# Gate and up products of all experts as float32 products in halves of TensorE's columns, weights unsplit, a ring of six slots

## The chip, the cores and the metric

The kernel runs on one core of a Trainium2 chip. A core has TensorE (PE; PEld is its loading of stationary tiles), VectorE (DVE), ScalarE (ACT), GpSimd (POOL) and a queue that issues loads (SP). The metric is the device time of one execution in microseconds (us); the median of the runs shown for the kernel before is 1627.42 us.

## What is computed

Two transformer blocks on 256 tokens of width 1024, all in float32. The first ends in a mixture of 32 experts (width 512, weights `w1`, `w3`, `w2`), the second block has two layers, each ending in a mixture of 16 experts (width 256). Each token goes to two experts. Cut to what matters here:

```python
# first block: 32 experts, D_FF_EXPERT = 512
return (jax.nn.silu(xb @ w1[e]) * (xb @ w3[e])) @ w2[e]
# second block, both layers: 16 experts, D_EXPERT = 256
a = jax.nn.silu(t @ w_gate[e]) * (t @ w_up[e])
out = out + combine[:, e:e + 1] * (a @ w_down[e])
```

In front of each mixture stand a norm, the routing and the mixer of the layer; between the first mixture and the last stand a latent attention and a long convolution, whose filters (the functions with `filter` in their names) are computed early, while the first mixture runs.

## The kernel before

Each expert has room for 64 tokens (`CAP`); what does not fit goes through a loop at the end (`overflow`), taken only where an expert has more. I call the stage of the 32 experts the wide stage and the other two the narrow stages.

**Streaming.** The weights come through a ring of slots, each 2 MB (128 partitions x 4096 float32). In the wide stage an expert takes three: gate, up, and half of the down weights of an earlier pair of experts. A narrow expert's gate and up share one slot, and a pair's down weights take one. `Stream.get` hands out a slot and issues the loads that are due, on SP's queue. The ring has four slots (the wide one uses one more place once, at the start).

**Gather.** For four experts at a time (`GE`) a product with a one-hot matrix picks their tokens, in 8 pieces of the contraction (`gather`, L254). The tokens are kept as a high and a low part, side by side: 64 columns of high and 64 of low make the 128 columns of a stationary tile.

**Gate and up.** A unit is two pieces of the contraction of one weight matrix, 512 columns each. `split` makes the high part of the weights on ScalarE (L272) and the low part on VectorE (L274); `mm` then runs four float32r products for a unit (L280). The result has the high tokens' and the low tokens' share in separate rows; `turn` (L307) adds them and transposes, in four float32 products with a 128x64 matrix `S`. Then come `silu` (L315) and the product with the up half, `act` (L322).

**Down and out.** The down product (L357) runs two experts at once: each has 64 tokens, and one expert's go to the lower, the other's to the upper half of the array's columns, as float32 products straight from the ring. `out_hi` (L364) and `out_lo` (L371) weight and split the result, `scatter` (L379) adds it to the tokens with a float32r product. `slots` (L334) makes the matrix for that.

**Order.** In `run` the order of all this is written by hand: `seq` lists the units, and a table (`LATE`, `OUT`, `OUTL`, `END`) says after how many further units each follow-up stands. The products' split runs `LA` = 2 units ahead. All other work, the filter rounds of the long convolution among it (L1630, L1649, L1657 on TensorE, sixteen rounds), is put between by a scheduler. Products of the mixture share three PSUM banks (`bank`), the filter rounds have one (`fill`).

Of the kernel before, what the change touches and what calls it, by code (L numbers as in the profile page):

```python
# [31 lines left out]
XG = 10  # L32
PRW, PRN = 2, 2
LA = 2
# [53 lines left out]
def make_consts(k):  # L88
# [15 lines left out]

    k.S = k.t(c, [P, CAP], F32, "S")
    nc.vector.tensor_tensor(k.S, k.ident[:, :CAP], k.ident[:, CAP:], op=ALU.add)
# [121 lines left out]
class Moe:  # L228


    def __init__(self, k, es, name, r, h2h, h2l, load, NE, FF):
        self.k, self.nc, self.r = k, k.nc, r
        self.h2h, self.h2l = h2h, h2l
        self.load = load
        self.NE, self.FF, self.name = NE, FF, name
        self.sb = es.enter_context(k.pool(name + "sb", 2))
        self.acc = [[k.acc() for h in range(2)] for t in range(2)]
        self.first = True
        self.xg, self.oh, self.st = {}, {}, {}
        self.prime = PRW if FF == 512 else PRN  # L240
# [5 lines left out]
    def gather(self, g, c, oh=None, n=None):  # L246
# [3 lines left out]
        pm = k.bank()  # L250
# [5 lines left out]
        self.gp = pm  # L256
        return i

    def gathered(self, g, c, n=None):
        k, nc, pm = self.k, self.nc, self.gp  # L260
        n = n or GE
        N = n * CAP
        xg = k.t(self.sb, [P, n, 2, CAP], F32R, "xg", bufs=XG)
        self.gathers = nc.scalar.activation(xg.rearrange("p e a s -> p a e s"),  # L264
                             pm[:, :2 * N].rearrange("p (a e s) -> p a e s", a=2, e=n), AF.Copy)
        self.xg[g][c] = xg
# [10 lines left out]
    def mm(self, out, lhs, parts, start, stop):  # L277
        for j in range(2):
            for a, w in enumerate(parts):
                self.nc.tensor.matmul(out, lhs[j].bitcast(w.dtype), w[:, j, :], start=(start and j == 0 and a == 0),  # L280
                                      stop=(stop and j == 1 and w is parts[-1]))
# [4 lines left out]
    def x_of(self, e, c):  # L286
        g, i = divmod(e, GE)
        return self.xg[g][c][:, i].rearrange("p a s -> p (a s)")

    def up_unit(self, e, kind, u, parts):  # L290
# [6 lines left out]
    def evac(self, e, kind):  # L297
        s = self.state(e)
        s["s" + kind] = self.k.t(self.sb, [P, 512], F32, "s" + kind)
        self.nc.scalar.activation(s["s" + kind], s["p" + kind], AF.Copy)  # L300

    def turn(self, e, kind, c0, n):
# [6 lines left out]
        s["t" + kind] = pm  # L309

    def silu(self, e):
        s = self.state(e)
        n = self.FF // P
        s["sg"] = self.k.t(self.sb, [P, n * CAP], F32, "sg")
        self.nc.scalar.activation(s["sg"], s["tg"][:, :n * CAP], AF.Silu)  # L315

    def act(self, e):
        s, k, nc = self.state(e), self.k, self.nc
        n = self.FF // P
        pu = s["tu"][:, :256] if self.FF == 512 else s["tg"][:, n * CAP:2 * n * CAP]  # L320
        s["av"] = k.t(self.sb, [P, n, CAP], F32, "a", bufs=3)
        nc.vector.tensor_tensor(s["av"].rearrange("p c s -> p (c s)"), pu, s["sg"], op=ALU.mult)  # L322
# [62 lines left out]
    def overflow(self, add):  # L385
# [4 lines left out]
        with k.tc.If(r.nblk > 0):  # L390
            with k.tc.For_i(0, r.nblk, 1):
# [34 lines left out]
                x_of = lambda c: self.xg[g][c][:, 0].rearrange("p a s -> p (a s)")  # L426

                def units(kind, u):
                    w = k.t(self.sb, [P, 2, 512], F32, "wh", bufs=LA + 2)
# [3 lines left out]
                for kind in ("g", "u") if wide else ("g",):  # L433
                    s["p" + kind] = k.bank()
                    for u in range(4):
                        self.mm(s["p" + kind], [x_of(2 * u), x_of(2 * u + 1)], self.split(units(kind, u)), u == 0, u == 3)
                    self.evac(e, kind)
                    self.turn(e, kind, 0, 4)
                    if kind == "g":
                        self.silu(e)  # L440
# [29 lines left out]
    def start(self, oh):  # L470

        self.onehot(0, oh)
        with self.k.tc.issue_after(self.low.ins):
            self.parts = {("g", 0, u): self.split(self.load("g", 0, u)) for u in range(self.prime)}
        with self.k.tc.issue_after(self.high.ins):
            for c in range(8):
                self.ready = self.gather(0, c)
                self.gathered(0, c)

    def run(self):  # L480
# [4 lines left out]
        LATE = (1, 2, 3, 3) if wide else (2, 2, 3, 4)  # L485
        OUTL = (1, 2, 4) if wide else (1, 1, 4)
        END, OUT = (0, 0, 0, 0), (1, 2, 4) if wide else (1, 1, 4)
        seq = []
        for i in range(NE + 2):
            if i < NE:  # L490
                for kind in ("g", "u") if wide else ("g",):
                    seq += [(kind, i, u) for u in range(4)]
# [9 lines left out]
        for e in range(NE):  # L502

            late = END if e == NE - 1 else LATE
            for kind in ("g", "u") if wide else ("g",):
                n = where[kind, e, 3]
                lt = LATE if kind == "g" and wide else late
                add(n + lt[0], self.evac, e, kind)
                add(n + lt[1], self.turn, e, kind, 0, 4)
                if kind == "g":  # L510
                    add(n + lt[2], self.silu, e)
                if kind == "u" or not wide:
                    add(n + lt[3], self.act, e)
            ge = where["g", e, 3]
            if e % 2 == 0:
                n = ge if wide else ge - 1
                add(n, self.slots, e // 2)
                add(n + 1, self.slots_out, e // 2)
                for h in range(2):
                    d = where["d", e // 2, h * nck + nck - 1]  # L520
                    o = OUTL if e == NE - 2 else OUT
                    add(d + o[0], self.out_hi, e // 2, h)
                    add(d + o[1], self.out_lo, e // 2, h)
                    add(d + o[2], self.scatter, e // 2, h)
        for g in range(1, NE // GE):
            el = g * GE - 1
            last = "u" if wide else "g"
            early = XG - 8
            add(where[last, el - 1, 0], self.onehot, g)
            ns = [where[last, el - 1, 1 + c] for c in range(early)]  # L530
# [1830 lines left out]
```

## Time and profile before

| | us |
|---|---|
| median of 3 runs (lowest to highest) | 1627.42 (1626.41 to 1630.23) |
| the profiled execution, its own time | 1621.13 |
| its span, first to last instruction | 1619.4 |
| wide stage, first gate product to the last pair's down product | 336.27 to 925.12 |
| first narrow stage | 1114 to 1251 |
| second narrow stage | 1469 to 1608 |

The page gives busy time by engine, what ended an engine's idle time, and the queues. A record of TensorE is one pass as the profiler wrote it: a float32r product is one record, a float32 product is two. A record's duration includes the time that its result takes to come through, so records overlap; the price of one is read from the distance of starts. Times of a group are the union of its records. In a window's row the engines stand as PE, PEld, DVE, ACT, POOL, then the granted clock of TensorE; in a group's row the idle time behind the second bar is that of the engine just before the group's instructions, with what ended it.

### The profile page before, as it was taken

To read this page: it belongs to the slowest core of one execution; us is meant where nothing else is said; L and a number is where in the kernel's file an instruction comes from. 1 tells how busy PE (TensorE), PEld (TensorE's weight loads), DVE (VectorE), ACT (ScalarE), POOL (GpSimd) and SP (SyncE) were. 2 spreads that over 40 slices of the span, in tenths; PEclk is the share of its full clock that TensorE was granted. 3 is DMA by queue.
4 is the path that set the end of the run, shared out by engine and by line. 5 is a ranking of instruction groups with operands and counts; after the bars stand their busy time and mean duration, and the time that the engine had idled before them with its cause. 6 is when DMAs were issued, how large, how long until landed. Compare 5 with 4: busy or idle time off the path is not lost. (4 is left out here: it accounts for less than half of the span.)

```text
span 1619.4 us, 20894 instructions
## 1 busy us (share of the span) xinstructions
PE 1477.1 (91%) x7754; PEld 1014.0 (63%) x7754; DVE 1004.8 (62%) x1935; ACT 889.6 (55%) x1413; POOL 70.5 (4%) x98
## 2 busy tenths in 40 slices
PE   5898999889999999999999969997999799878997
PEld 2675586666665666666666544656676678556764
DVE  3553564687657565656565567447775768567665
ACT  2462343476666666666656444436775534337774
POOL 0000000110000000000000000001000000010000
PEclk8899999989999999999999989997999899978999
DMA  8557714658988889888889667665997674475994
GB/s 326 177 169 239 258 44 143 273 223 321 370 342 327 349 316 358 319 347 329 333 340 384 278 257 282 211 245 226 355 366 298 244 268 154 131 299 196 365 362 155
DMA packets 67789, 444.48 MB, mean 274 GB/s; under 512 B 7813, under 2 KB 8165, under 8 KB 43744
## 3 DMA queue, kind: packets, MB, share of 16 engines
q1 hardware_dynamic: 61712, 424.97, 69.4%
q0 software_dynamic: 5536, 17.37, 3.0%
q8 instruction: 63, 1.03, 0.3%
q10 hardware_dynamic: 432, 0.72, 0.1%
q14 instruction: 46, 0.38, 0.1%
HBM read 437.75 MB, written 5.29 MB: 274 GB/s over the span
## 5 line engine op out<-in xcount | busy, mean ns | idle before, releaser
L274 DVE TENSOR_TENSOR wl<-ring,wh 128x1024 fp32r<-128x1024 f32 x384 | 454.4, 1220 | 130.8 <-ACT wh L272 129.2
L272 ACT ACTIVATE wh<-ring 128x1024 fp32r<-128x1024 f32 x384 | 386.1, 1053 | 14.3 <-DVE h2l L1926 13.3
L280 PE MATMUL bank<-wl,xg 128*128 128x512 f32 x768 | 315.6, 411 | 16.2 <-DVE wl L274 16.1
L280 PE MATMUL bank<-wh,xg 128*128 128x512 f32 x768 | 311.2, 405 | 3.0 <-ACT wh L272 3.0
L280 PEld LDWEIGHTS bank<-wl,xg 128*128 128x128 f32 x768 | 145.4, 189 | 72.0 <-DVE wl L274 42.5
L357 PE MATMUL bank<-ring,a 128*64 128x512 f32 x768 | 188.6, 605 | 0.0
L280 PEld LDWEIGHTS bank<-wh,xg 128*128 128x128 f32 x768 | 145.8, 190 | 42.6 <-issue 14.6
L812 DVE TENSOR_TENSOR wl<-ra,wh 128x1024 fp32r<-128x1024 f32 (+1 forms) x77 | 93.5, 1216 | 81.3 <-ACT wh L810 69.2
L810 ACT ACTIVATE wh<-ra 128x1024 fp32r<-128x1024 f32 (+1 forms) x77 | 80.7, 1054 | 111.1 <-PE acc L825 38.1
L264 ACT ACTIVATE xg<-bank 128x512 fp32r<-128x512 f32 x128 | 75.5, 597 | 58.2 <-PE bank L254 56.1
L357 PEld LDWEIGHTS bank<-ring,a 128*64 128x64 f32 x768 | 47.6, 136 | 74.4 <-issue 61.6
L893 PE MATMUL fill<-rb,cpad 128*32 128x512 f32 x384 | 84.5, 620 | 8.1 <-DMA rb<-in_w_mod_dram 4.5
L307 PEld LDWEIGHTS bank<-S,sg 128*128 128x128 f32 x512 | 65.1, 191 | 18.1 <-ACT wh L272 11.4
L307 PE MATMUL bank<-S,sg 128*128 128x64 f32 x512 | 66.2, 272 | 0.4 <-ACT sg L300 0.2
L364 ACT ACTIVATE o_h<-bank,gt 128x512 fp32r<-128x512 f32 x64 | 43.7, 683 | 36.1 <-PE bank L357 36.1
L254 PE MATMUL bank<-oh,h2h 128*128 128x256 f32 x256 | 60.6, 322 | 3.1 <-DVE oh L222 2.5
L315 ACT ACTIVATE sg<-bank 128x256 f32<-128x256 f32 (+1 forms) x64 | 21.2, 332 | 71.1 <-PE bank L307 68.6
L1632 DVE TENSOR_TENSOR hd<-fill,dec 128x512 f32<-128x512 f32 x16 | 11.0, 690 | 79.2 <-PE fill L1630 79.2
L254 PEld LDWEIGHTS bank<-oh,h2h 128*128 128x128 f32 x256 | 46.6, 210 | 17.3 <-ACT xg L264 6.9
L1683 PE MATMUL acc<-hTh,wh 128*128 128x256 f32 x192 | 56.0, 293 | 0.0
L1683 PE MATMUL acc<-hTl,wh 128*128 128x256 f32 x192 | 55.9, 293 | 0.0
L254 PE MATMUL bank<-oh,h2l 128*128 128x256 f32 x256 | 54.8, 300 | 0.6 <-DVE h2l L1926 0.6
(666 smaller groups left out, 2526.0 us busy)
## 6 DMA issues: line engine op xcount, KB each, us to landing
ring<-in_w_dram SPq DMA_DIRECT2D x64, 2048.0 KB, 9.0
ring<-in_moe_w_in_dram SPq DMA_DIRECT2D x32, 2048.0 KB, 9.6
ring<-in_w_dram SPq DMA_DIRECT2D x62, 1024.0 KB, 8.2
rb<-in_ada_w_dram SPq DMA_DIRECT2D x96, 512.0 KB, 4.6
ring<-in_moe_w_down_dram SPq DMA_DIRECT2D x32, 1024.0 KB, 9.0
rb<-in_w_mod_dram SPq DMA_DIRECT2D x32, 512.0 KB, 4.5
ra<-in_hy_w_in_dram SPq DMA_DIRECT2D x12, 1024.0 KB, 6.9
ra<-in_w_in_dram SPq DMA_DIRECT2D x20, 512.0 KB, 3.7
```

The costliest lines, as they stand in the source:

```text
L254: i = nc.tensor.matmul(pm[:, a * N:(a + 1) * N], h[:, t, c * P:(c + 1) * P], oh[:, t], start=(t == 0), stop=(t == 1))
L264: self.gathers = nc.scalar.activation(xg.rearrange("p e a s -> p a e s"), pm[:, :2 * N].rearrange("p (a e s) -> p a e s", a=2, e=n), AF.Copy)
L272: self.high = nc.scalar.activation(wh, w, AF.Copy)
L274: nc.vector.tensor_tensor(wl, w, wh.bitcast(F32), op=ALU.subtract)
L280: self.nc.tensor.matmul(out, lhs[j].bitcast(w.dtype), w[:, j, :], start=(start and j == 0 and a == 0), stop=(stop and j == 1 and w is part ...
L307: self.nc.tensor.matmul(pm[:, c * CAP:(c + 1) * CAP], s["s" + kind][:, c0 + c * P:c0 + (c + 1) * P], k.S, start=True, stop=True)
L357: self.nc.tensor.matmul(q["d", h][i * CAP:(i + 1) * CAP], self.state(2 * p + i)["av"][:, c], w[:, i], start=(c == 0), stop=(c == nk - 1))
L364: nc.scalar.activation(oh[r], s["d", h][r], AF.Copy, scale=s["gt"][r])
L810: k.last[0] = k.nc.scalar.activation(wh[:, :, :n], w, AF.Copy)
L812: k.last[1] = k.nc.vector.tensor_tensor(wl[:, :, :n], w, wh[:, :, :n].bitcast(F32), op=ALU.subtract)
L893: nc.tensor.matmul(pr[32 * g:32 * g + 32], k.cpad[:, l, 2 * q + i], wq[:, i], start=(r == 0), stop=(r == 1))
L1683: nc.tensor.matmul(acc[i][:, :T], y[:, jj, i * P:(i + 1) * P], self.hT[x][:, kt], start=(kt == 0 and a == 0), stop=(kt == 7 and a == 2))
```

## The change

Gate and up become float32 products. For each piece of the contraction the same stationary tile, 64 columns of unsplit tokens, is used twice: for the gate weights into rows 0 to 63 of a PSUM bank, that is into the lower half of the array's columns, and for the up weights into rows 64 to 127, the upper half. The weights are read from the ring as they are; `split` and `mm` are gone, and with them `LA`, the primed units at the start, and the `wh` and `wl` buffers. The host lays `w1` and `w3` out together as `w13`, so that a slot of the wide ring holds gate and up of half an expert's contraction.

The gather adds high and low in PSUM (four products into the same columns), and evicts two pieces at a time. One `evac` and one `turn` serve gate and up: four 128x128 transposes in the wide stage, two in the narrow ones. The order table is replaced: eviction right after an expert's last unit, turn, silu and act two units later, gather pieces one per unit in the last two experts of a group. The rings have six slots in all three stages. Padding and sides of some buffers change.

```diff
     def gather(self, g, c, oh=None, n=None):
...
+        o = c % 2 * 256
+        if o == 0:
+            self.gp = k.bank()
         for a, h in enumerate((self.h2h, self.h2l)):
             for t in range(2):
-                i = nc.tensor.matmul(pm[:, a * N:(a + 1) * N], h[:, t, c * P:(c + 1) * P],
-                                     oh[:, t], start=(t == 0), stop=(t == 1))
+                i = nc.tensor.matmul(self.gp[:, o:o + N], h[:, t, c * P:(c + 1) * P],
+                                     oh[:, t], start=(a == t == 0), stop=(a == t == 1))
...
-    def split(self, w):
-        k, nc = self.k, self.nc
-        wh = k.t(self.sb, [P, 2, 512], F32R, "wh", bufs=LA + 2)
-        self.high = nc.scalar.activation(wh, w, AF.Copy)
-        wl = k.t(self.sb, [P, 2, 512], F32R, "wl", bufs=LA + 2)
-        nc.vector.tensor_tensor(wl, w, wh.bitcast(F32), op=ALU.subtract)
-        return wh, wl
...
+    def up_unit(self, e, u, w, x_of=None):
         s = self.state(e)
         if u == 0:
-            s["p" + kind] = self.k.bank()
-        self.mm(s["p" + kind], [self.x_of(e, 2 * u + j) for j in range(2)], parts, u == 0, u == 3)
+            s["p"] = self.k.bank()
+        for j in range(2):
+            c = 2 * u + j
+            x = x_of(c) if x_of else self.x_of(e, c)
+            for a in range(2):
+                self.nc.tensor.matmul(s["p"][a * CAP:(a + 1) * CAP, :self.FF], x, w(a, c), start=(c == 0), stop=(c == 7))
...
-        for c in range(n):
-            self.nc.tensor.matmul(pm[:, c * CAP:(c + 1) * CAP], s["s" + kind][:, c0 + c * P:c0 + (c + 1) * P], k.S,
-                                  start=True, stop=True)
+        for c in range(self.FF // P):
+            self.nc.tensor.transpose(pm[:, c * P:(c + 1) * P], s["s"][:, c * P:(c + 1) * P], k.ident)
...
+            add(n, self.evac, e)
+            m = n + (0 if last else 2)
+            add(m, self.turn, e)
+            add(m, self.silu, e)
+            add(m, self.act, e)
...
-RINGS = {'m1': 3, 'n0': 4, 'n1': 4}
+RINGS = {'n0': 6, 'n1': 6}
...
-            ring = [ph(f"ring{i}") for i in range(4)]
...
+            ring = [ph(f"ring{i}") for i in range(4)] + [ph(f"ring{i}", side="right") for i in range(4, 6)]
+            S = Stream(k, es, "ring", 6, 4096, homes=[ring[int(c)] for c in RO])
```

How the order moves, on TensorE early in the wide stage, before: gate and up units of an expert (`bank` from `wh`, `wl` and the gathered `xg`), then a turn (`S`, `sg`).

```order
L280 MATMUL bank_3226<-wh_3201,xg_2919 128x512
L280 MATMUL bank_3226<-wl_3203,xg_2919 128x512
L280 MATMUL bank_3226<-wh_3211,xg_2926 128x512
L280 MATMUL bank_3226<-wl_3213,xg_2926 128x512
L280 MATMUL bank_3226<-wh_3211,xg_2933 128x512
L280 MATMUL bank_3226<-wl_3213,xg_2933 128x512
L307 MATMUL bank_3249<-S_72,sg_3231 128x64 x4
```

Here each product waits for its split, and a turn follows for each kind. The same place now: L283 are gate and up together (two pieces, two halves), L251 the gather, L295 the turn.

```order
L283 MATMUL bank_3011<-ring_2743,xg_2939 64x512 x4
L283 MATMUL bank_3047<-ring_2745,xg_2906 64x512 x4
L251 MATMUL bank_3052<-oh_3016,h2h_2749 128x256 x2
L251 MATMUL bank_3052<-oh_3016,h2l_2750 128x256 x2
L283 MATMUL bank_3047<-ring_2745,xg_2917 64x512 x4
L295 MATMUL bank_3061<-ident_60,s_3042 128x128 x4
```

Products of a half array and products of the whole array now alternate, and a turn has four instructions for gate and up together.

The filter rounds on TensorE in the wide stage, before (L1649, L1630 and L1657 write `fill`; L280 are gate and up):

```order
L1649 MATMUL fill_7056<-ident_60,fs_7044 128x128 x2
L1649 MATMUL fill_7056<-ident_60,fd_7045 128x128 x2
L1630 MATMUL fill_7067<-fh_6995,w_1822_7063 128x256 x2
L1657 MATMUL fill_7084<-ftk_7061,dftf_6987 128x128 x2
L280 MATMUL bank_3687<-wh_3669,xg_3268 128x512
L1657 MATMUL fill_7084<-ftk_7061,dftf_6987 128x128 x4
L280 MATMUL bank_3687<-wl_3671,xg_3268 128x512
L280 MATMUL bank_3687<-wh_3669,xg_3279 128x512
L280 MATMUL bank_3687<-wl_3671,xg_3279 128x512
L280 MATMUL bank_3687<-wh_3677,xg_3381 128x512
```

Here the parts of a round stand between products of whole columns. The same part of a round now (L1608, L1589 and L1616 are the same three lines; L363 is the scatter, with `acc` the sum over experts):

```order
L1608 MATMUL fill_5243<-ident_60,fd_5220 128x128 x2
L1589 MATMUL fill_5254<-fh_5102,w_1172_5250 128x256 x2
L283 MATMUL bank_3479<-ring_3347,xg_3345 64x512 x4
L283 MATMUL bank_3479<-ring_3347,xg_3376 64x512 x4
L363 MATMUL acc_2894<-o_h_3472,sc_3236 128x512
L363 MATMUL acc_2894<-o_l_3474,sc_3236 128x512
L363 MATMUL acc_2896<-o_h_3472,sc_3236 128x512
L363 MATMUL acc_2896<-o_l_3474,sc_3236 128x512
L1616 MATMUL fill_5271<-ftk_5248,dftf_5094 128x128 x8
L283 MATMUL bank_3479<-ring_3378,xg_3427 64x512 x4
```

The parts of a round lie between blocks of half-array products; the sixteen rounds stand in experts 5 to 18 of the program, where they stood in 5 to 25.

On ScalarE in the wide stage, before (`wh` the high part of weights, `su` and `sg` evictions and silu, `xg` the gather's eviction):

```order
L300 ACTIVATE su_3284<-bank_3226 128x512
L272 ACTIVATE wh_3295<-ring_3155 128x1024
L272 ACTIVATE wh_3303<-ring_3155 128x1024
L272 ACTIVATE wh_3309<-ring_3155 128x1024
L1746 ACTIVATE fh_6995<-fd_7006 64x256
L364 ACTIVATE o_h_3318<-bank_3281,gt_3050 128x512
L272 ACTIVATE wh_3320<-ring_3155 128x1024
```

Passes over weights fill the row here. The same place now (`s` is the eviction of gate and up, `sc` that of the slots):

```order
L348 ACTIVATE o_h_3201<-bank_3183,gt_3006 128x512
L288 ACTIVATE s_3234<-bank_3208 128x512
L328 ACTIVATE sc_3236<-bank_3227 128x256
L301 ACTIVATE sg_3253<-bank_3248 128x256
L348 ACTIVATE o_h_3261<-bank_3243,gt_3098 128x512
```

An expert's passes over weights are gone from the row.

## Rows read from the trace of the kernel before

**Rows 1.** Page, part 1: busy us by engine, share of the span, instructions

```profile
PE 1477.1 (91%) x7754; PEld 1014.0 (63%) x7754; DVE 1004.8 (62%) x1935; ACT 889.6 (55%) x1413; POOL 70.5 (4%) x98
```

**Rows 2.** Windows: length, busy us (records) by engine, clock, DMA share, GB/s

```profile
336.00:400.00 64.00, 61.49 (x302) 43.51 (x301) 51.53 (x71) 53.58 (x75) 2.31 (x4) 1.00 0.78 304
400.00:870.00 470.00, 447.51 (x2252) 299.55 (x2250) 292.96 (x398) 296.87 (x447) 29.12 (x46) 1.00 0.90 341
...
1114.00:1251.00 137.00, 134.82 (x681) 92.66 (x680) 92.76 (x124) 100.26 (x147) 0.00 (x0) 1.00 0.85 325
...
1469.00:1608.00 139.00, 136.07 (x682) 93.93 (x681) 92.78 (x124) 101.92 (x148) 0.00 (x0) 0.99 0.78 303
```

**Rows 3.** Groups, 400:880 us: xcount | busy us, mean ns | idle

```profile
L274 DVE TENSOR_TENSOR wl<-ring,wh 128x1024 fp32r<-128x1024 f32 x200 | 235.3, 1219 | 67.0 <-ACT wh L272 66.8
L272 ACT ACTIVATE wh<-ring 128x1024 fp32r<-128x1024 f32 x201 | 201.5, 1051 | 0.5 <-PE bank L280 0.4
L280 PE MATMUL bank<-wl,xg 128*128 128x512 f32 x398 | 167.4, 421 | 11.8 <-DVE wl L274 11.8
L280 PE MATMUL bank<-wh,xg 128*128 128x512 f32 x399 | 161.6, 405 | 1.6 <-ACT wh L272 1.6
L357 PE MATMUL bank<-ring,a 128*64 128x512 f32 x400 | 98.2, 606 | 0.0
L1657 PE MATMUL fill<-ftk,dftf 128*128 128x128 f32 x256 | 34.6, 281 | 7.8 <-DVE hd L1632 7.8
...
L1630 PE MATMUL fill<-fh,w 64*128 64x256 f32 x64 | 20.9, 420 | 0.7 <-ACT ftk L1651 0.7
```

**Rows 4.** Timeline of TensorE, wide stage: start us, us, what (merged where alike)

```profile
599.47 1.94 PE L357 MATMUL bank<-ring,a 128*64 128x512 f32 x8
601.34 1.10 PE L307 MATMUL bank<-S,su 128*128 128x64 f32 x8
602.37 1.94 PE L357 MATMUL bank<-ring,a 128*64 128x512 f32 x8
...
605.20 0.39 PE L280 MATMUL bank<-wh,xg 128*128 128x512 f32 x1
605.43 0.40 PE L280 MATMUL bank<-wl,xg 128*128 128x512 f32 x1
```

**Rows 5.** Timeline, end of the wide stage: the last pair's down product

```profile
925.12 3.65 PE L357 MATMUL bank<-ring,a 128*64 128x512 f32 x16
...
926.04 0.14 PEld L357 LDWEIGHTS bank<-ring,a 128*64 128x64 f32 x2 [0.29 <-issue]
926.47 0.14 PEld L357 LDWEIGHTS bank<-ring,a 128*64 128x64 f32 x2 [0.29 <-issue]
```

**Rows 6.** Timeline before the wide stage: transposes of 128 columns

```profile
311.61 0.82 PE L1761 MATMUL acc<-ident,xres 128*128 128x128 f32 x6
```

**Rows 7.** Timeline of TensorE: the last gather products and the first gate product

```profile
336.03 0.40 PE L254 MATMUL bank<-oh,h2l 128*128 128x256 f32 x2
336.27 0.41 PE L280 MATMUL bank<-wh,xg 128*128 128x512 f32 x1
```

**Rows 8.** Windows as above, of 10 us, late in the wide stage

```profile
890.00:900.00 10.00, 9.72 (x47) 7.07 (x45) 8.83 (x10) 6.38 (x9) 0.00 (x0) 1.00 1.02 418
900.00:910.00 10.00, 10.00 (x47) 6.05 (x47) 7.39 (x8) 8.70 (x11) 0.00 (x0) 1.00 0.97 402
```

**Rows 9.** Waits of SP's queue, 360:900 us: us in total, times, longest

```profile
SPq L1823 <- PE bank L357: 191.8, 28, 10.5
SPq L1823 <- DVE wl L274: 137.7, 28, 8.1
```

**Rows 10.** Timeline of TensorE, attention: float32 products of 256 columns on the whole array

```profile
1016.47 0.59 PE L1558 MATMUL sc<-knT,qnT 128*128 128x256 f32 x2
1016.90 0.59 PE L1559 MATMUL sc<-kpe,qpT 128*128 128x256 f32 x2
```

More of the change, by code (lines that the diff above doesn't have):

```diff
@@ L425, in overflow @@
                     self.gathered(g, c, 1)
-                x_of = lambda c: self.xg[g][c][:, 0].rearrange("p a s -> p (a s)")
+                x_of = lambda c: self.xg[g][c]
                 def units(kind, u):
-                    w = k.t(self.sb, [P, 2, 512], F32, "wh", bufs=LA + 2)
+                    w = k.t(self.vpool, [P, 2, 512], F32, "vw", bufs=2)
                     self.fetch(w, kind, ereg, u)
                     return w
[L433 to L440, printed above, removed]
+                for u in range(4):
+                    if wide:
+                        w2 = [units(kind, u) for kind in "gu"]
+                        w = lambda a, c: w2[a][:, c % 2]
+                    else:
+                        w1 = units("g", u)
+                        w = lambda a, c: w1[:, c % 2, a * 256:(a + 1) * 256]
+                    self.up_unit(e, u, w, x_of)
+                self.evac(e)
+                self.turn(e)
+                self.silu(e)
                 self.act(e)
@@ L472, in start @@
         self.onehot(0, oh)
[L473 to L478, printed above, removed]
+        for c in range(8):
+            self.ready = self.gather(0, c)
+            self.gathered(0, c)
     def run(self):
@@ L490, in run @@
             if i < NE:
-                for kind in ("g", "u") if wide else ("g",):
-                    seq += [(kind, i, u) for u in range(4)]
+                seq += [("g", i, u) for u in range(4)]
             for h in ([i % 2] if wide else [0, 1][:2 - i % 2 * 2]) if i >= 2 else []:
@@ L502, in run @@
         for e in range(NE):
[L504 to L513, printed above, removed]
@@ L514, in run @@
-            ge = where["g", e, 3]
+            n = where["g", e, 3]
+            last = e == NE - 1
+            add(n, self.evac, e)
[3 more added lines that the diff above has]
+            add(m, self.act, e)
             if e % 2 == 0:
-                n = ge if wide else ge - 1
-                add(n, self.slots, e // 2)
-                add(n + 1, self.slots_out, e // 2)
+                add(n - 1, self.slots, e // 2)
+                add(n, self.slots_out, e // 2)
@@ L527, in run @@
[L527 to L530, printed above, removed]
-            ns += [where[last, el, 0] + c for c in range(8 - early)]
+            add(where["g", g * GE - 3, 0], self.onehot, g)
             for c in range(8):
-                add(ns[c], self.gather, g, c)
-                add(ns[c] + 1, self.gathered, g, c)
-        parts = self.parts
-        done = self.prime
+                n = where["g", g * GE - 2 + c // 4, c % 4]
+                add(n, self.gather, g, c)
+                add(n, self.gathered, g, c)
@@ L537, in run @@
         for n, (kind, e, u) in enumerate(seq):
-            while done < min(n + 1 + LA, len(seq)):
-                w = self.load(*seq[done])
-                if seq[done][0] == "d":
-                    parts[seq[done]] = w
-                else:
-                    parts[seq[done]] = self.split(w)
-                done += 1
-            p = parts.pop((kind, e, u))
             if kind == "d":
-                self.down_unit(e, *divmod(u, nck), nck, p)
+                self.down_unit(e, *divmod(u, nck), nck, self.load(kind, e, u))
```

105 lines of the change are left out of this document (38 added, 67 removed).

## The prediction

> **What bounds the kernel now.** I read the stage windows first, then the groups of instructions in the long stretch, then the order of single instructions there, and last the waits of the DMA queue.
>
> The page's busy shares [rows 1] put TensorE first, with VectorE and ScalarE behind it; shares over the whole span say little, so the stages come next. The windows [rows 2] split the span: the first mixture of experts (the "wide" one, 32 experts) runs from 336 to about 925 us, the two "narrow" ones from 1114 to 1251 and from 1469 to 1608. The change touches these three alone. TensorE is busy for 448 of 470 us in the long stretch of the wide one, and all but 2 or 3 us of the narrow ones. DMA is not full: 341 GB/s at 0.90 there, 325 and 303 in the narrow stages.
>
> Why is TensorE not faster? In the stretch from 400 to 880 us [rows 3] there are 797 float32r products of gate and up. An expert has 32 of them (2 kinds, 8 chunks of the contraction, high and low half of the weights), so 24.9 experts passed in 480 us, **19.3 us each**. VectorE and ScalarE make the two halves of the weights in the same stretch (235 and 202 us), and the products waited 11.8 and 1.6 us outright for them. The queue that loads the ring waited for slots, not for the memory: for its gate and up loads 192 us until a product was done with a slot and 138 us until the split was [rows 9]. So compute sets the pace; the loads follow.
>
> **What an expert costs TensorE, before.** Prices from the order in time [rows 4]: a float32r product of 512 columns every 0.23 us (605.20, 605.43); a block of four float32 down products, written as 8 records, 1.87 us (599.47 to 601.34); a turn (4 float32 products of 64 columns, 8 records) 1.03 us (601.34 to 602.37). A gather product takes 0.12 us (two in 336.03 to 336.27 [rows 7]). Per wide expert: 32 x 0.229 = 7.33 for gate and up; two turns 2.06; two down blocks 3.74; four scatter products 0.93; a quarter of 32 gather products 0.95; slots 0.1. Sum **15.1 us**. The filter rounds of the next block (16 of them, scheduled into this stage) cost about 4.0 each: 4 records of L1630 at 0.32 (20.9 us over 64 [rows 3]), 16 of L1657 at 0.11, 4 transposes, and some breaks; 64 in all. Over 24.9 experts that is 15.1 + 2.6 = 17.7; the missing 1.6 us of the 19.3 are waits, 40 us in the stretch. For the stage, first gate product (336.27 [rows 7]) to the start of the last pair's down products (about 920; its second half starts at 925.12 [rows 5]), 583 us: 32 x 15.1, less 9 for the first two experts, which have no down product beside them, plus 64 is 538, so some 45 us of waits.
>
> **The change, step by step.** *Gate and up.* 32 float32r products become 16 float32 ones, each on 64 columns of the array, which the trace shows as 32 records, as it does for the down products that already have this form. How such a pair runs is in the weight loads of the down products [rows 5]: two records (one in each half of the array) start together, the next two 0.43 us later (926.04, 926.47). So 0.215 a record, 32 x 0.215 = 6.88, hardly less than 7.33: **the arithmetic itself is not the gain.** Going into and out of the half-array form costs: 8 records are 1.72, the block took 1.87, so 0.15 a run. Up and down products now have the same form and join: a wide expert has about 2.5 runs (broken by scatter, turn and, for every second, slots), 0.38.
>
> *Turns.* 16 records become 4 transposes of 128 columns. Six transposes of that shape took 0.82 us with the last one's 0.27 in it [rows 6]: 0.11 each, 0.44 for 4, against 2.06. This is the largest sure term, **1.6 us an expert**.
>
> *Gather.* The same 32 products, half the evictions. But each of the 8 pieces now breaks a run of up products: 8 x 0.15 a group of four, 0.3 an expert.
>
> *Sum after:* 6.88 + 3.44 (down, 16 x 0.215) + 0.38 + 0.44 + 0.93 + 0.95 + 0.3 + 0.1 = **13.4 us**, for the stage 32 x 13.4 - 9 + 16 x 3.9 = 483, against 538: 55 us less work.
>
> *The split.* 256 passes of 1.05 us on ScalarE and 1.22 on VectorE go in the wide stage, and with them the products' waits for them. What remains of the 45 us lies between 0 (nothing left) and 80 (the filter rounds, in the program's order now in experts 5 to 18 and not 5 to 25, wait for ScalarE and VectorE about twice as densely). I take **25**: the nearest rows are the products' idle time for the split, 13.4 us named outright [rows 3], with knock-ons about half of the 45, and the rest is the rounds' and the three PSUM banks'. Around a gather all three banks are held when the down product starts (gate and up, slots or gather, gather), and it waits for the 0.6 us eviction behind a 0.5 us gather: 0.4 us, eight times, within the 25. Wide stage: 483 + 25 = 508, **75 us less**.
>
> *The ring.* Six slots of 2 MB, freed by the product itself and no longer by the split; two experts of lead. Bytes: 96 slots of 2.1 MB, six of them loaded before the first product, and 16 rounds of 0.45 MB: 196 MB. At the 402 to 418 GB/s that the ring reached where it ran free [rows 8] that is 479 us, from the first slot freed at about 340 on: 819, while TensorE would end near 845. The loads are hidden, by 25 us. If that cover is gone, the loads' time is what ends last. The load of the overflow count on SP's queue moves behind the last ring load; it ends some 10 us before the stage does and costs nothing.
>
> *Narrow stages.* Per pair of experts before: 7.33 + 3.74 + 2.06 + 1.86 + 1.9 + 0.2 = 17.1, and 137 us over 8 pairs is 17.1 [rows 2]: hardly a wait. After: 64 records of 256 columns. On half an array no such row exists; on the whole one, two records of a 256-column float32 product take 0.43 us (1016.47 to 1016.90 [rows 10]), so side by side 0.108 a record, 6.9. Down 3.44, transposes 0.44, scatter 1.86, gather 1.9, slots 0.2, runs 5 x 0.15 plus 4 x 0.15 for gathers 1.35: 16.1. **1.0 us a pair, 8 us a stage, 16 for both**; between 6 (more breaks) and 24 for both. The order of work at their start (norm, routing, gather) is the same, and the two more slots only lengthen the lead.
>
> **Sum.** 75 + 16 = 91. The profiled execution took 1621.1 us, 6.3 under the median of 1627.4; both give the same step, so 1530 by that execution and **1536** by the median.
>
> **Rivals.** *Waits eat it.* The rounds, packed into 13.5 experts of 18 us, make TensorE wait in order: one round alone has three visits to TensorE around one PSUM bank. With 80 us of waits the wide stage is 563, 20 less, in all 36: 1591. For it: more rounds per expert in the new order. Against it: ScalarE and VectorE, for which they wait, lose half their work.
>
> *The loads bind.* If the ring cannot pass the 341 GB/s of the long stretch [rows 2], 196 MB take 575 us: the last lands at 915, as now, the wide stage gains 7, in all 23: 1604. Against it stand the 10 us stretches at 402 to 418 [rows 8] and a queue that waited for slots [rows 9]. The Trainium skill (DMA: Bandwidth & Descriptors, Where 436 GB/s comes from) says that for loads from HBM the memory side binds at about 358 GB/s per core; at that rate the wide stage would end at 888, which gives about 1579. This trace disagrees, with 418.
>
> *Slower: the halves do not overlap.* If the two products of a chunk, which have the same stationary tile, or 256 columns, ran one after the other, each step of two records would take 0.43 us more in the wide stage (512 steps) and 0.215 in the narrow (512 steps): 330 us, 1627 - 91 + 330 = 1866. It decides from 91 / 1024 = 0.09 us a step. Against it: the down products in the same half-array form load their weights together, two loads within 0.14 us [rows 5].
>
> *Better.* No wait at all and two runs fewer: 483 in the wide stage, in all 115 to 124: about 1508.
>
> **How the numbers follow.** Forecast (waits of 10 to 45 us) 0.62, from 1515 to 1570; better 0.11; waits eat it 0.13; the loads bind 0.06; slower 0.06; the rest, gain and loss that cancel, 0.02. Eight in ten: the forecast's own stretch, most of "better", and the near half of the waits: 1507 to 1588. A difference of under 0.2% (3 us) this kernel's runs cannot tell from none. Faster 0.91, same 0.02, slower 0.07.
>
> **What would show it.** The gate and up products in pairs that start together, pairs 0.43 us apart (0.22 in the narrow stages); an expert of about 13.4 us outside the filter rounds and 18 within; turns of 0.44 us; DMA near 400 GB/s in the wide stage; the wide stage ending near 845 to 850 us, the narrow ones 8 us shorter. It is wrong if the products wait for the ring, if TensorE stands before filter rounds for over 3 us each, if a break costs much more than 0.15 us, or if the granted clock, 1.00 in these stages now [rows 2], falls there.

## The result, and the profile after

The changed kernel takes **1575.9 us** (median of 4 runs, 1571.86 to 1578.06) where the kernel before takes 1627.8: a ratio of 0.9677, 95% interval 0.9652 to 0.9701, or 52 us less. The forecast was 1536, 91 us less. The time lies inside the stated range (1507 to 1588) and outside the forecast's own stretch (1515 to 1570), on the way to the rival in which waits eat it (1591).

Where the time went is seen by cutting both profiled executions at the first gate product and the last scatter product of each stage (starts read from TensorE's rows; "lead-in" is what lies between two stages):

| us | before | after | gain | forecast |
|---|---|---|---|---|
| wide stage | 595.2 | 548.0 | 47.2 | 75 |
| lead-in of the first narrow stage | 182.3 | 193.4 | -11.0 | 0 |
| first narrow stage | 139.8 | 134.1 | 5.7 | 8 |
| lead-in of the second | 215.3 | 213.8 | 1.5 | 0 |
| second narrow stage | 141.7 | 135.4 | 6.3 | 8 |
| span | 1619.4 | 1570.0 | 49.4 | 91 |

So the miss is in two places: 28 us too little in the wide stage and 11 us lost where nothing was expected. The page's first part, which answers to [rows 1], shows that VectorE and ScalarE lost about half of their work, and that TensorE stays at 90%:

```profile
PE 1417.5 (90%) x7690; PEld 806.7 (51%) x7690; DVE 568.9 (36%) x1550; ACT 468.8 (30%) x933; POOL 70.6 (4%) x98
```

The windows (columns as in [rows 2]): 420 to 700 is the stretch with the filter rounds, 700 to 860 the one behind them, the last two are the narrow stages.

```profile
420.00:700.00 280.00, 262.06 (x1248) 122.57 (x1248) 51.77 (x144) 62.34 (x148) 26.73 (x42) 0.99 0.86 321
700.00:860.00 160.00, 159.82 (x742) 60.79 (x740) 16.74 (x40) 27.09 (x52) 0.00 (x0) 1.00 1.01 425
1078.00:1212.00 134.00, 132.72 (x848) 70.83 (x848) 23.42 (x73) 32.09 (x72) 0.00 (x0) 1.00 0.87 331
1425.00:1561.00 136.00, 133.40 (x855) 71.37 (x855) 23.11 (x65) 34.08 (x74) 0.00 (x0) 1.00 0.77 293
```

Behind the rounds the ring moves 425 GB/s and TensorE has no gap; inside them it moves 321, less than the 341 of [rows 2], and TensorE stands for 18 of 280 us. The groups of that stretch (columns as in [rows 3]):

```profile
L283 PE MATMUL bank<-ring,xg 128*64 128x512 f32 x428 | 104.1, 614 | 0.0
L341 PE MATMUL bank<-ring,a 128*64 128x512 f32 x208 | 62.8, 606 | 0.0
L1616 PE MATMUL fill<-ftk,dftf 128*128 128x128 f32 x254 | 36.0, 283 | 3.1 <-DVE hd L1591 3.1
L1589 PE MATMUL fill<-fh,w 64*128 64x256 f32 x56 | 16.1, 404 | 6.8 <-ACT ftk L1610 6.8
```

Gate and up (L283) wait for nothing any more; the waits that are left belong to the rounds, whose parts share one PSUM bank. The waits of TensorE over nearly the whole stage, 340 to 880 us (us in total, times, longest; L1608 are a round's transposes):

```profile
PE fill L1608 <- ACT hd L1619: 8.0, 11, 0.8
PE fill L1589 <- ACT ftk L1610: 7.5, 10, 1.0
PE fill L1616 <- DVE hd L1591: 5.3, 5, 2.2
```

These are 20.8 us in 26 waits. 428 records of gate and up, 32 an expert, are 13.4 experts in 280 us, **20.9 us each**. Before it was 19.3 [rows 3], over a stretch in which the rounds were thinner. Behind the rounds four experts take 56.0 us (starts of every 32nd record of L283: 15.6, 15.2, 12.9, 12.3), 14.0 each. The expert without a round is near the 13.4 of the sum; the rounds are not near their price.

Why, the order in time shows. One down product of four steps, torn by a round (the same view as [rows 4]; L1616 is a part of a round, L341 the down product, L295 the turn):

```profile
515.05 0.38 PE L1616 MATMUL fill<-ftk,dftf 128*128 128x128 f32 x2
515.36 1.07 PE L341 MATMUL bank<-ring,a 128*64 128x512 f32 x2
516.37 0.49 PE L1616 MATMUL fill<-ftk,dftf 128*128 128x128 f32 x2
516.78 1.93 PE L341 MATMUL bank<-ring,a 128*64 128x512 f32 x6
518.65 0.66 PE L295 MATMUL bank<-ident,s 128*128 128x128 f32 x4
519.23 1.94 PE L341 MATMUL bank<-ring,a 128*64 128x512 f32 x8
```

The product of one half stands alone (2 records from 515.36, 1.01 us until the next start) and then 6 records take 1.87 us, as long as the 8 of an untorn block at 519.23. In the wide stage 13 such pairs are torn (26 of its runs hold an odd number of half-array products). A second thing is seen in the narrow stage: a whole-array visit between half-array products.

```profile
1132.44 0.39 PE L363 MATMUL acc<-o_l,sc 128*128 128x512 f32 x1
1132.76 1.08 PE L283 MATMUL bank<-ring,xg 128*64 128x256 f32 x8
1133.78 0.50 PE L251 MATMUL bank<-oh,h2h 128*128 128x256 f32 x2
1134.12 0.39 PE L251 MATMUL bank<-oh,h2l 128*128 128x256 f32 x2
1134.44 1.08 PE L283 MATMUL bank<-ring,xg 128*64 128x256 f32 x8
```

The 8 records take 1.02 us instead of 8 x 0.108 = 0.86, which is the 0.15 that the prediction counted; but the four gather products between them take 0.66 instead of 4 x 0.12 = 0.48. A visit costs on both sides, 0.34 us in all here.

The third loss is in front of the first narrow stage (timeline of all engines; `srow` and `shrow` are the modulation rows that the tokens need before routing):

```profile
1043.75 0.57 POOL L813 DMA_DIRECT2D shrow<-mrows  x1 [44.39 <-ACT sqj L732]
...
1044.04 1.29 SPq L1786 DMA_DIRECT2D ring<-in_moe_w_in_dram  x3
...
1044.31 0.54 POOL L813 DMA_DIRECT2D srow<-mrows  x1
...
1045.51 1.30 SPq L1795 DMA_DIRECT2D ring<-in_moe_w_down_dram  x2
...
1060.85 4.64 POOL L1737 TENSOR_TENSOR h<-xres,srow 128x1024 f32<-128x1024 f32 x2 [16.00 <-DMA srow<-mrows]
...
1068.38 0.17 PE L159 MATMUL bank<-n0Ab,before 128*128 128x16 bf16 x1 [19.20 <-DVE n0Ab L155]
```

The rows are asked for at 1044, in the midst of six slots of weights, and land 16.5 us later; TensorE stands for 19 us. The first ring load had itself waited, 20.9 us of SP's queue for the last residual (`xres`, L795). Before, nothing waited for this load, and TensorE stood for 5 us at the same place.

### The profile page after: what moved, and what is told of

Same layout as the page of the kernel before. It is cut to its first block, busy times and chain, and to the rows that moved or that the text cites. A ratio compares the mean times of both kernels' runs of the same rounds, so it can differ in the third digit from the quotient of the medians.

```text
span 1570.0 us, 19641 instructions
## 1 busy us (share of the span) xinstructions
PE 1417.5 (90%) x7690; PEld 806.7 (51%) x7690; DVE 568.9 (36%) x1550; ACT 468.8 (30%) x933; POOL 70.6 (4%) x98
## 3 DMA queue, kind: packets, MB, share of 16 engines
q8 instruction: 63, 1.03, 0.3%
## 5 line engine op out<-in xcount | busy, mean ns | idle before, releaser
L283 PE MATMUL bank<-ring,xg 128*64 128x512 f32 (+1 forms) x2048 | 373.5, 498 | 0.0
L283 PEld LDWEIGHTS bank<-ring,xg 128*64 128x64 f32 x2048 | 132.5, 137 | 156.3 <-issue 117.9
L341 PE MATMUL bank<-ring,a 128*64 128x512 f32 x768 | 199.8, 602 | 0.2
L306 DVE TENSOR_TENSOR a<-bank,sg 128x256 f32<-128x256 f32 (+1 forms) x64 | 22.8, 356 | 308.6 <-ACT sg L301 172.5
L288 ACT ACTIVATE s<-bank 128x512 f32<-128x512 f32 (+1 forms) x64 | 31.4, 491 | 264.0 <-PE bank L283 264.0
L341 PEld LDWEIGHTS bank<-ring,a 128*64 128x64 f32 x768 | 52.8, 136 | 82.6 <-issue 75.6
L355 DVE SCALAR_TENSOR_TENSOR o_l<-bank,gt,o_h 128x512 fp32r<-128x512 f32 x64 | 48.0, 751 | 81.1 <-ACT o_h L348 80.5
L262 ACT ACTIVATE xg<-bank 128x512 f32<-128x512 f32 x64 | 38.3, 598 | 130.2 <-PE bank L251 129.9
L251 PEld LDWEIGHTS bank<-oh,h2h 128*128 128x128 f32 x256 | 43.7, 208 | 47.2 <-issue 40.5
L251 PE MATMUL bank<-oh,h2h 128*128 128x256 f32 x256 | 63.0, 331 | 4.3 <-DVE oh L217 4.3
L363 PE MATMUL acc<-o_h,sc 128*128 128x512 f32 x128 | 57.2, 447 | 0.8 <-ACTq L374 0.8
L251 PE MATMUL bank<-oh,h2l 128*128 128x256 f32 x256 | 54.2, 298 | 0.7 <-DVE h2l L1879 0.7
L1642 PE MATMUL acc<-hTh,wl 128*128 128x256 f32 x192 | 54.6, 289 | 0.2 <-DVE wl L771 0.2
L363 PE MATMUL acc<-o_l,sc 128*128 128x512 f32 x128 | 50.6, 395 | 1.8 <-DVE o_l L355 1.8
L301 ACT ACTIVATE sg<-bank 128x256 f32<-128x256 f32 (+1 forms) x64 | 21.1, 329 | 97.1 <-PE bank L295 97.0
## 6 DMA issues: line engine op xcount, KB each, us to landing
ring<-in_w_dram SPq DMA_DIRECT2D x64, 2048.0 KB, 11.1
```

Source lines behind the costliest of these rows:

```text
L251: i = nc.tensor.matmul(self.gp[:, o:o + N], h[:, t, c * P:(c + 1) * P], oh[:, t], start=(a == t == 0), stop=(a == t == 1))
L262: self.gathers = nc.scalar.activation(xg, self.gp.rearrange("p (a s) -> p a s", a=2)[:, :, :n * CAP], AF.Copy)
L283: self.nc.tensor.matmul(s["p"][a * CAP:(a + 1) * CAP, :self.FF], x, w(a, c), start=(c == 0), stop=(c == 7))
L288: self.nc.scalar.activation(s["s"], s["p"][:, :self.FF], AF.Copy)
L341: self.nc.tensor.matmul(q["d", h][i * CAP:(i + 1) * CAP], self.state(2 * p + i)["av"][:, c], w[:, i], start=(c == 0), stop=(c == nk - 1))
L355: nc.vector.scalar_tensor_tensor(ol[r], s["d", h][r], s["gt"][r], oh[r].bitcast(F32), op0=ALU.mult, op1=ALU.subtract)
```

## The experiments

All were timed against the kernel before on the same chip; times are medians. What a kernel gains on the changed one is the difference of the two ratios, times 1627.8 us, since the kernel before ran at 1624 to 1628 us from one set of runs to the next; stage lengths and starts are from the profiled execution of each. None of them leaves out any work.

**Four slots in the first narrow stage alone.**

```diff
-RINGS = {'n0': 6, 'n1': 6}
+RINGS = {'n0': 4, 'n1': 6}
```

> The ring of the first narrow stage has four slots again, all else is as in the changed kernel. In the changed kernel 193.4 us lie between the last scatter of the wide stage and the first gate product of the first narrow stage, against 182.4 before; TensorE stands for 19 us there while the modulation rows (srow), issued only after five of six ring loads, land 16.5 us later. Theory A (the six slots take the room in which the rows were loaded early, so the rows come behind 12 MB of weights): the rows are issued ahead of the ring again, the lead-in is 180 to 183 us, the total about 1565 (11 less than 1576). Rival (the attention stage itself became slower, by sharing the memory with other loads): lead-in 193, total 1576. If the narrow stage needs the two slots it grows beyond its 134.1 us.

1559.7 us (ratio 0.9605, interval 0.9587 to 0.9622), 12 less than the changed kernel. In the profiled execution the lead-in is 183.4 us and the stage 134.07, as short as with six slots. The rows are asked for at 979.62, where nothing waits for them yet, and the ring's loads go out from 1026.53 on. When the rows are wanted, what POOL waits for is the last residual (L1720), and no load:

```profile
1045.97 2.36 POOL L1737 TENSOR_TENSOR h<-xres,srow 128x1024 f32<-128x1024 f32 x1 [43.33 <-PE acc L1720]
```

Theory A holds in place and size: 10 us of the lead-in (the rows had stood between the ring loads, not behind five of them, as the expectation put it). In the five kernels here with six slots in this stage the lead-in is 192.6 to 197.8 us, in the two with four in this stage alone 183.4 and 183.1. The lead-in of the second narrow stage, where nothing was changed, was 5.7 us shorter too; the granted clock over that stretch was 0.91, against 0.89 in the changed kernel. Across all kernels here it lies between 208 and 217 us, so a few us of any single total are its wandering.

**Two gather pieces at a time.**

```diff
-                n = where["g", g * GE - 2 + c // 4, c % 4]
+                n = where["g", g * GE - 2 + c // 4, c % 4 | 1]
```

> Two gather pieces stand together after every second unit, instead of one after each; the same instructions. Runs of half-array products in the program fall from 144 to 124 in the wide stage and from 55 to 46 in each narrow one. Theory B (a visit of the whole array between half-array products costs 0.35 us beside its products, as the starts in the trace suggest): 38 visits x 0.35 = 13 us less, 1563, and each narrow stage 3.2 us shorter. Rival (0.15 us a visit, as the prediction had it): 5.7 us less, 1570, the narrow stages 1.35 us shorter each. Rival (the loads set the pace of the wide stage): the wide stage does not move, only the narrow ones do.

1556.7 us (ratio 0.9574, 0.9549 to 0.9598), 17 less. The narrow stages, where only the visits changed, are 130.97 and 132.31 us long: 3.1 us less each for 9 visits, **0.345 us a visit**, on the price of theory B and over twice that of the prediction. The wide stage fell by 11.1 us, more than 20 visits x 0.35 = 7: the scheduler put the rounds elsewhere too, and their waits in the stage are 15.7 us instead of 20.8, at one torn pair more (14). The pieces in the narrow stage now:

```profile
1131.24 0.40 PE L251 MATMUL bank<-oh,h2h 128*128 128x256 f32 x2
1131.48 0.40 PE L251 MATMUL bank<-oh,h2l 128*128 128x256 f32 x2
1131.72 0.40 PE L251 MATMUL bank<-oh,h2h 128*128 128x256 f32 x2
1131.95 0.40 PE L251 MATMUL bank<-oh,h2l 128*128 128x256 f32 x2
1132.29 1.95 PE L283 MATMUL bank<-ring,xg 128*64 128x256 f32 x16
```

The second piece starts every 0.24 us without a loss, and 16 records run in 1.87 us without a break.

**The filter rounds by hand.** The rounds are made into parts that the written order calls; `plan` says behind which unit:

```diff
+            for n in range(19):
+                e = 3 + n
+                d = ("d", (e - 2) // 2, e % 2 * 4 + 1)
+                for key, i in ((("g", e, 1), n - 3), (("g", e, 3), n - 1), (d, n - 2), (d, n)):
+                    if 0 <= i < 16:
+                        plan.setdefault(key, []).append(units[i])
...
             for f, a in at.pop(n, []):
                 f(*a)
+            for part in plan.get((kind, e, u), []):
+                next(part)
```

Two things more differ from the changed kernel: the parts are set up before the mixture's products are written, and the rounds' table `dec` has two buffers instead of one.

> The sixteen filter rounds are put into the written order by hand, one per expert from expert 3 on, each part directly behind a scatter, a gather or a turn, never between the two halves of a down pair, with at least one unit of products between two parts of a round; its loads are issued one expert earlier. Theory C (a round costs 6.3 us in the changed kernel since 13 down pairs are torn apart, at 0.9 to 1.0 us each, since 1.4 us of each round are waits for the one bank, and since parts make visits of their own): a round costs about 3.3 us, the wide stage falls from 548 to about 500 us, the total to about 1528. Rival (the loads set the pace of the wide stage, 196 MB at 425 GB/s being 461 us from 340 on): TensorE gets free earlier but the ring is waited for; the wide stage stays above 535 and the gain is under 13 us. Rival (ScalarE and VectorE set the price of a round): about 1570.

1525.5 us (ratio 0.9392, 0.9374 to 0.9410), 46 less than the changed kernel with the same number of instructions on TensorE, VectorE and ScalarE; the wide stage is 500.2 us. The window over the stretch with the rounds:

```profile
400.00:720.00 320.00, 319.91 (x1628) 150.99 (x1628) 64.06 (x177) 78.18 (x179) 27.13 (x43) 1.00 0.99 399
```

TensorE has no gap and the ring moves 399 GB/s. A part now stands right behind the turn, in the same visit:

```profile
551.93 0.66 PE L295 MATMUL bank<-ident,s 128*128 128x128 f32 x4
552.43 0.38 PE L1612 MATMUL fill<-ident,fs 128*128 128x128 f32 x2
552.65 0.38 PE L1612 MATMUL fill<-ident,fd 128*128 128x128 f32 x2
552.96 1.94 PE L341 MATMUL bank<-ring,a 128*64 128x512 f32 x8
```

Four experts with four rounds take 69.4 us (18.8, 18.5, 16.3, 15.8), without them 56.0: **3.35 us a round**. The 47.8 us between the two wide stages are 3.0 for each of sixteen rounds, so a round costs 6.3 in the changed kernel. Theory C holds in its total; how much each of its causes takes is worked out further below. Both rivals fall, the loads' because TensorE never waits for the ring in that stretch. The second buffer of `dec` does not explain the gain: in the changed kernel VectorE waited for that table once, 2.3 us.

**Gate, gate, up, up.** Within a unit the two loops change places, so that the two gate products come first.

```diff
-        for j in range(2):
-            c = 2 * u + j
-            x = x_of(c) if x_of else self.x_of(e, c)
-            for a in range(2):
+        for a in range(2):
+            for j in range(2):
+                c = 2 * u + j
+                x = x_of(c) if x_of else self.x_of(e, c)
```

> In each unit the two gate products come first and then the two up products (g g u u in place of g u g u); the same instructions. Theory D (two half-array products overlap only where they stand next to each other in the program): a unit of four takes 3 x 0.86 = 2.6 us instead of 1.72 if the second gate and the first up product still overlap, +0.86 for 128 wide and +0.43 for 128 narrow units: 165 us more, 1741; without any overlap 330 more, 1906. Rival (the array runs the halves side by side whatever the order): no change, 1576.

1578.6 us (two runs; ratio 0.9719, 0.9690 to 0.9748; the changed kernel 0.9652 to 0.9701): 7 us more at the middle of both intervals, which overlap, where theory D had 165 or 330. It falls. The stages are 3.3 and twice 0.9 us longer, some 0.02 us for each of 256 units, and a unit still takes 1.87 us:

```profile
744.57 1.94 PE L283 MATMUL bank<-ring,xg 128*64 128x512 f32 x8
746.44 0.51 PE L363 MATMUL acc<-o_h,sc 128*128 128x512 f32 x1
```

So two products of different halves need not stand next to each other to share their time within a run. What tears a pair would then be the product of the whole array between them, which the next run tests.

**A part between the two halves of a down pair.** As the rounds by hand, but the transposes of each round stand inside `down_unit`:

```diff
         for i in range(2):
+            for part in mid if i else ():
+                next(part)
             self.nc.tensor.matmul(q["d", h][i * CAP:(i + 1) * CAP], self.state(2 * p + i)["av"][:, c], w[:, i],
```

> As by_hand (1525.5 us, wide stage 500.2 us), but the four transposes of each of the sixteen rounds stand between the two halves of a down pair instead of behind the turn. The run with g g u u showed that the order within a run of half-array products does not matter. Theory E (a product of the whole array empties the array first, so a half whose partner stands behind it runs its 0.86 us alone): 16 x (0.86 + a visit of 0.35) = 19 us more, wide stage 519, total 1545. Rival (the partner catches up later, as it does within a run): only the visit, 16 x 0.35 = 6 us, total 1531.

1544.0 us (ratio 0.9501, 0.9475 to 0.9527), 18 more than the rounds by hand. The wide stage is 518.6 us, 18.4 more, 1.15 us for each of sixteen rounds:

```profile
561.01 1.93 PE L343 MATMUL bank<-ring,a 128*64 128x512 f32 x6
562.88 0.44 PE L1614 MATMUL fill<-ident,fs 128*128 128x128 f32 x2
563.15 0.38 PE L1614 MATMUL fill<-ident,fd 128*128 128x128 f32 x2
563.46 1.07 PE L343 MATMUL bank<-ring,a 128*64 128x512 f32 x2
564.47 0.66 PE L295 MATMUL bank<-ident,s 128*128 128x128 f32 x4
```

6 records for 1.87 us and 2 for 1.01, as in the changed kernel at 515.36. Theory E holds. The Trainium skill (TensorEngine Tiling (Array Packing), Tiling Modes) says that a change of the tiling mode drains TensorE and that tiles of one mode run independently; the gathers in pairs and this run agree with the first (0.345 us for a visit, 1.15 us for a torn pair), and the run with g g u u with the second (1.87 us a unit in either order).

**Four slots everywhere.** `RINGS` at four for both narrow stages, and `ring` with four places in the wide one.

```diff
-            ring = [ph(f"ring{i}") for i in range(4)] + [ph(f"ring{i}", side="right") for i in range(4, 6)]
-            S = Stream(k, es, "ring", 6, 4096, homes=[ring[int(c)] for c in RO])
+            ring = [ph(f"ring{i}") for i in range(4)]
+            S = Stream(k, es, "ring", 4, 4096, homes=[ring[int(c)] for c in RO])
```

> The changed kernel with rings of four slots in all three stages. Theory F (the ring's depth carries little: the loads keep 425 GB/s wherever a slot is free, and the lead is used up only where TensorE takes more than that): the wide stage grows by up to 10 us from 548, the lead-in of the first narrow stage falls by 10 as in n0_four, total 1565 to 1576. Rival (the six slots carry a good part of the gain): the wide stage grows by 30 us or more, total 1595 or above.

1567.9 us (ratio 0.9648, 0.9622 to 0.9675), 5 us *less* than with six in the middle, though the intervals overlap: at the least, six slots everywhere gain nothing on four. The wide stage grew by 9.5 us to 557.5, the lead-in of the first narrow stage fell by 17.1 to 176.3, that of the second grew by 3.0. Theory F holds for the wide stage; the lead-in fell by 7 us more than it named. There TensorE's wait of 9.0 us for the rows that VectorE makes (`xn`), which the changed kernel and the run with four slots in the first narrow stage have in this lead-in, is missing; why, no run shows. Where the 9.5 us are is seen behind the rounds, in the window from 720 to 880: the loads are full, and TensorE stands for 5 us.

```profile
720.00:880.00 160.00, 154.89 (x690) 57.79 (x686) 16.18 (x38) 24.65 (x48) 0.00 (x0) 1.00 1.01 425
```

The groups of the same stretch say for what it stands, the ring's loads:

```profile
L283 PE MATMUL bank<-ring,xg 128*64 128x512 f32 x352 | 82.6, 600 | 3.2 <-DMA ring<-in_w_dram 3.1
```

An expert takes 14.75 us there (mean of four, 13.3 to 15.7), which is its 6.29 MB at 426 GB/s; with six slots it takes 14.0, living off the lead.

**The kernel before, its rounds by hand.** The same kind of edit on the kernel before, one round an expert, the parts behind gate and up units, without the ring's one-time place; `dec` keeps its one buffer.

> The kernel before, with its sixteen filter rounds put in by hand one per expert from expert 3 on (and without the ring's one-time place, whose room the rounds' buffers take). Theory G (what the rounds cost beyond their work in the changed kernel comes from torn pairs and visits, which the kernel before, with float32r products on the whole array, hardly has): the gain is under 20 us, 1605 to 1625. Rival (the scheduler's placing costs the kernel before as much, 47 us): about 1577.

1622.4 us (ratio 0.9979, 0.9963 to 0.9996): 3 us less. Theory G holds. Four experts with four rounds take 80.0 us there (21.1, 22.4, 18.5, 18.0), without them 64.0: 4.0 us a round, as the prediction had priced it, and 16.0 an expert, 2.0 more than after the change.

**Rounds by hand, gathers in pairs, four slots in the first narrow stage.**

> by_hand, gather_pairs and n0_four together. If the three are independent: 1525.5, less 7 in the wide stage (20 visits at 0.35), 6 in the narrow ones, 10 in the lead-in of the first narrow stage: about 1502. Rival (the loads bind the wide stage from here: by_hand already moves 410 GB/s there): the wide stage stays at 500 and the total is 1509.

**1501.3 us** (1499.85 to 1502.90; ratio 0.9245, 0.9223 to 0.9266), 70 less than the changed kernel. The wide stage is 492.7 us, 7.4 less than with the rounds by hand for 21 runs fewer, 0.35 a visit once more; the narrow stages 130.97 and 132.3, the lead-in 183.1. The three parts add up, and the loads, at 400 GB/s over the wide stage, do not bind yet.

## Why the prediction went as it did

**What held.** The products of two halves run side by side, 0.43 us a pair, so the arithmetic is no gain; the turns are. The rival in which the halves don't overlap (1866) is refuted, and with g g u u they overlap even where the two products of a chunk do not follow each other. The granted clock stayed at 0.99 to 1.00 in the three stages. The loads ran at 425 GB/s and stayed hidden, so "the loads bind" (1604) fell too. The Trainium skill (DMA: Bandwidth & Descriptors, Where 436 GB/s comes from) has the memory side bind at about 358 GB/s a core; this trace has 425 over 160 us on the one core in use, which decides. The waits were put at 25 us for the wide stage; TensorE's outright waits for the rounds are 20.8 us (1.3 a round, under the 3 that would have been a sign of being wrong), so that term was near, though the 3 us that it held for the banks around the gathers did not come up.

**The step that failed first: the price of a run of half-array products.** The working took 0.15 us from the block of down products, 1.87 against 8 x 0.215 [rows 4], and stopped there. It looked at the half-array side alone. The other side was in the same rows: the turn between two such blocks took 1.03 us for 8 records at 0.11, which is 0.15 too much, and the working put that down as the turn's price. A visit costs 0.35 (0.345 by the gathers in pairs), and so the prediction's own sign of being wrong, a break much dearer than 0.15 us, came up. The traces have 143 runs of half-array products in the wide stage and 54 in each narrow one (the expectations count one more of each in the program), 67 and 15 before. The prediction's 4.5 runs an expert in the wide stage are 3.9 behind the rounds, its 9 a pair in the narrow ones 6.8: it counted too many and priced them far too low. For the narrow stages that is the whole miss in the middle of the stage: 54 x 0.35 is 8 us more than 72 x 0.15, so 1.0 a pair; a pair of experts was forecast at 16.1 us and takes 17.2 (34.5 for four experts, starts of every 64th record), against 17.3 before. What the narrow stages gained, 12 us of 16, they gained mostly at their two ends, where the prediction had named no gain, so that 12 stands near 16 by luck.

**The second: the rounds at 3.9 us.** They were priced by their work before, where a part stands among products of the whole array. That price is right there (4.0 in the kernel before, by hand) and would have been enough after (3.35, by hand). What the working did not see is that the new order puts parts between the halves of a down pair, though the order of the changed kernel was there to be read. A round came to 6.3. Of the 3.0 us more than by hand, 1.3 are waits for the one bank (20.8 us in sixteen rounds), 0.9 torn pairs (13 at 1.15), 0.1 further visits (143 runs against 124, 13 of them from torn pairs: 6 at 0.35). The last 0.6 a round, some 10 us in all, no experiment places. By my estimate 4 of them belong to the waits: a wait is counted from the end of the record before it, and a 128x128 record lasts 0.27 us where the next could have started after 0.11, 26 times. "Waits eat it" was the right rival for half its reason: it named the rounds, and their waits in order, but its 80 us of waits are 20.8, and it did not name the torn pairs.

For the wide stage the terms then are: an expert without a round 14.0 for 13.4, 32 x 0.6 = 19 us (3.9 runs at 0.35 are 0.7 more than the 0.68 that the sum has for them); the rounds with their waits 16 x 6.3 = 101 for 62 + 25, 14 us; less 4 us in the first two experts, which take 7.5 us each and so 13 less than two others, where the sum took off 9. That is 29, where 28 were missing.

**The third: the two slots that "only lengthen the lead".** They cost 10 to 11 us in front of the first narrow stage, by the run with four slots there. The time before the stage, which I counted on for filling the ring, was also the time of a small load that the stage needs first. That the rows come late because the six slots take room that is still in use is inferred from what POOL waited for (a square sum on ScalarE, 44.39 us), from SP's wait for the last residual, and from the order of the kernels; that the load then takes 16.5 us beside the ring is in the trace.

Together: 75 forecast, less 28; 16, less 4; and 11 lost make 48, or 49.5 with the 1.5 gained in the other lead-in; the span shows 49.4. The time fell inside the stated range because that range reached into the rival with the waits; the forecast's own stretch missed it by 6 us.

## What to carry to other kernels

When a product is cut into halves of the array, count the changes between half and whole in the new order before counting products: a visit of the whole array cost 0.35 us here, and work that is put between two halves cost some 0.8 us more than that (1.15 us in all), so fill-in work belongs next to other whole-array products. A small load that a stage needs first should be issued ahead of the stage's prefetch; here a deeper ring pushed it into the middle. And where a change halves other engines' load without the time following, look at what the scheduler now puts between the main products: the same instructions, placed by hand, gave nearly as much again as the change itself (46 us, and 52).

## What the runs showed of the hardware that I had not expected

- Changing from half-array to whole-array products and back costs 0.345 us beside the work, by 9 visits less in a stage; moving a round's four transposes out of such a visit to between the two halves of a pair costs 1.15 us, the visit of their own included.
- The order of products for the two halves within a run hardly matters: g u g u and g g u u both take 1.87 us a unit of four in the rows, and the stages differ by 0.02 us a unit.
- One core's loads held 425 GB/s for 160 us, and an expert's 6.29 MB then set its time (14.75 us) as soon as the ring was four slots deep.
- A load of modulation rows took 16.5 us to land beside a ring of six slots being filled; the same kernel's other two loads of this kind took 5.2 and 11.1 us, those of the kernel before 4.9 to 7.8 us.
